# Tying the loads, sums and stores of attention merges behind later work in a two-layer trunk kernel

## The chip, the cores and the metric

One core of one Trainium2 chip. The metric is device microseconds of one execution, as the median of several runs. Five engines work side by side: PE (matrix products), DVE (vector), ACT (scalar, activations), POOL (GpSimd) and SP, which here issues every DMA on one queue, in order.

## The reference

Two layers over 1024 rows of width 1024. Layer 0 is dilated attention, and only it is touched here; layer 1 (grouped attention with sinks) follows.

```python
def mixer_a(x, w_in, w_out, cos, sin):
    h = x @ w_in
    for gi, (window, dil) in enumerate(((128, 1), (512, 4), (2048, 16))):
        q, k, v = split_cols(h[..., base:base + 3 * A_WIDTH], [A_WIDTH] * 3)
        q = apply_rope(...); k = apply_rope(...)
        o, lse = banded_attention(strided(q), strided(k), strided(v), window // dil)
        outs.append(o); lses.append(lse)
    wts = jax.nn.softmax(jnp.stack(lses, axis=0), axis=0)
    o = jnp.einsum('gbsh,gbshd->bshd', wts, jnp.stack(outs, axis=0))
    z = h[..., -A_WIDTH:]
    return (o * jax.nn.silu(z)) @ w_out
```

The softmax over the three groups and the weighted sum of their outputs are what the kernel calls a merge.

## The kernel before

Every float32 product is done as three float16 products of high and low halves (lines 272 to 274): one row tile of 128 rows against a block of 512 weight columns is 24 matmuls into a tile `lin`. A weight block comes in four chunks `wraw`, its largest value is found (`wpm` L109 on DVE, then a small table `mdd` L230, which PE spreads over the rows at L237), and ACT (L132) and DVE (L133) split it into `whl`, four instructions each.

Layer 0 works in two halves of the heads (`pair` 0 and 1). In each half the groups come in the order 1, 2, 0, and for each group one block of values and two blocks of queries with keys, eight row tiles each. A value tile leaves PSUM through ACT (`vh` L368) and DVE (`vl` L369). A query tile goes through DVE (`t` L347, L350), POOL (`t` L351), ACT (`hl` L357), POOL (`hl` L358), ACT (L361) and a DMA transpose (`qk` L362). A unit of attention takes scores on PE (`s` L385), DVE (`sm`, `mx` L389), ACT (`st` L393, `sm` L395, `phl` L399), POOL or DVE (`phl` L401), a DMA transpose (`pT` L404), PE (`o` L416 to L418) and ACT (`st` L698). There is one PSUM tile for `o`, so the next unit's `o` waits for that eviction. The result goes to a scratch array in memory (`scr` L707), with its sums and its maxima.

When the last group of a half has written row tile n, `merge(n, pair, scr)` is queued. A merge is a generator in three parts: three loads of 264 KB into `gt` (L749); then the weights, on DVE (`mM` L754, `mw` L755, `mwl`, `mL`, `mw` L758 to L762) with one ACT exponential (`mw` L756) and three POOL instructions over 512 columns (`gt` L765 to L767); then two DVE instructions (L769, L770) and the store `oa` (L771). `merge_step` moves it on; at most two merges are under way, and `gt` has two buffers. There are eight merges in each half. Those of pair 0 fall into the end of its last group and the first group of pair 1. Those of pair 1 fall into its last query block and into the z blocks (gate columns; `zt`, `zu` L720 to L723, store `za` L729) which end the layer. Behind these comes the output projection: its weights `wo` are split (L132, L133) once the last store has left `gt`'s memory, and then `wg`, the weights of the next gate, are loaded and measured.

The order of instructions on each engine is not written out by hand. The framework's scheduler decides it from the program order and its own estimates, and an engine keeps that order: an instruction that waits holds up all behind it. `issue_after(ins)` adds one demand to it: what is issued inside stands behind `ins` on its engine.

Of the kernel before, what the change touches and what calls it, by code (L numbers as in the profile page):

```python
# [15 lines left out]
ALU = mybir.AluOpType  # L16
AX = mybir.AxisListType
# [3 lines left out]
P = 128  # L21
# [5 lines left out]
HD = 64  # L27
# [6 lines left out]
V_SHIFT = 25  # L34
# [105 lines left out]
class Trunk:  # L140
# [196 lines left out]
    def rope_out(self, ps, nq, nk, n, dst):  # L337

        nc, w = self.nc, self.work
        nh = nq + nk
        t1 = w.tile([P, 512], F32, tag="t1", name="t1")
        t2 = w.tile([P, 512], F32, tag="t2", name="t2")
        pv = ps.rearrange("p (h c) -> p h c", c=32)
        cos = self.cos[:, n, :].unsqueeze(1).to_broadcast([P, 2 * nh, 32])
        nc.vector.tensor_mul(t1[:, :nh * HD].rearrange("p (h c) -> p h c", c=32), pv, cos)  # L347
        pb = ps.rearrange("p (h b c) -> p h b c", b=2, c=32)[:, :, ::-1, :]
        sin = self.sin[:, n].unsqueeze(1).to_broadcast([P, nh, 2, 32])
        nc.vector.tensor_mul(t2[:, :nh * HD].rearrange("p (h b c) -> p h b c", b=2, c=32), pb, sin)  # L350
        nc.gpsimd.tensor_add(t1[:, :nh * HD], t1[:, :nh * HD], t2[:, :nh * HD])  # L351
        nb = nh + nk
        hl = w.tile([P, 12, P], F16, tag="hl", name="hl", bufs=3)
        rv = t1[:, :nh * HD].rearrange("p (h c) -> p h c", c=HD)

        def parts():
            nc.scalar.activation(hl[:, :nh, 0:HD], rv, AF.Copy)  # L357
            nc.gpsimd.tensor_sub(hl[:, :nh, HD:P], rv, hl[:, :nh, 0:HD])  # L358
            if nk:
                src, to = (hl[:, a:b, :].rearrange("p h (w c) -> p h w c", w=2) for a, b in ((nq, nh), (nh, nb)))  # L360
                nc.scalar.activation(to, src[:, :, ::-1, :], AF.Copy)  # L361
            nc.sync.dma_start(dst, hl[:, :nb, :].rearrange("p b c -> p (b c)"), transpose=True)  # L362

        self.ends.append(parts)

    def v_out(self, ps, vh, vl):
        nc = self.nc
        nc.scalar.activation(vh, ps, AF.Copy, scale=2.0 ** -V_SHIFT)  # L368
        nc.vector.scalar_tensor_tensor(vl, ps, 2.0 ** -V_SHIFT, vh, op0=ALU.mult, op1=ALU.subtract)  # L369


    def scores(self, qa, kas, mask, cs, ncs, sums, nbias, floor, pool_lo):

        nc, at = self.nc, self.att
        nb = len(kas)
        nk = nb * P
        sm = at.tile([P, 4, 2 * P], F32, tag="sm", name="sm", bufs=self.bufs)
        mx = self.small.tile([P, 4], F32, tag="mx", name="mx", bufs=6)
        for pr in range(2):
            ps = self.ps_s.tile([P, 2, 2 * P], F32, tag="s", name="s")  # L380
            for i in range(2):
                h = 2 * pr + i
                for kb, ka in enumerate(kas):
                    for sw in range(2):
                        nc.tensor.matmul(ps[:, i, kb * P:(kb + 1) * P], qa(h), ka(h, sw), start=(sw == 0),  # L385
                                         stop=(sw == 1))
            for i in range(2):
                h = 2 * pr + i
                nc.vector.tensor_tensor_reduce(sm[:, h, :nk], ps[:, i, :nk], mask, 1.0, -3e38, ALU.add, ALU.max,  # L389
                                               mx[:, h:h + 1])  # L390
        if floor is not None:
            nc.vector.tensor_max(mx, mx, floor)
        nc.scalar.activation(nbias, mx, AF.Copy, scale=ncs, bias=LN_PSCALE)  # L393
        for h in range(4):
            nc.scalar.activation(sm[:, h, :nk], sm[:, h, :nk], AF.Exp, bias=nbias[:, h:h + 1], scale=cs,  # L395
                                 accum_out=sums[:, h:h + 1])
        pf = at.tile([P, 16 * P], F16, tag="phl", name="phl", bufs=self.bufs)
        hl = pf[:, :8 * nk].rearrange("p (a h c) -> p a h c", a=2, h=4)
        nc.scalar.activation(hl[:, 0], sm[:, :, :nk], AF.Copy)  # L399
        eng = nc.gpsimd if pool_lo else nc.vector  # L400
        eng.tensor_sub(hl[:, 1], sm[:, :, :nk], hl[:, 0])  # L401
        pt = at.tile([P, 2, 4, 2, P], F16, tag="pT", name="pT", bufs=len(self.pipe))
        ptf = pt.rearrange("p a h b c -> p (a h b) c")[:, :8 * nb, :]
        nc.sync.dma_start(ptf, pf[:, :8 * nk], transpose=True)  # L404
        return ptf.rearrange("p (a h b) c -> p a h b c", a=2, h=4)

    def pv(self, pt, va, vla):
# [308 lines left out]
    def z_rows(self, pool, ps, c):  # L716

        nc = self.nc
        t = pool.tile([P, 512], F32, tag="t1", name="zt")
        nc.scalar.activation(t, ps, AF.Tanh, scale=c)  # L720
        u = pool.tile([P, 512], F32, tag="t2", name="zu")
        nc.scalar.activation(u, ps, AF.Copy, scale=c)  # L722
        nc.vector.scalar_tensor_tensor(u, t, 1.0, u, op0=ALU.add, op1=ALU.mult)  # L723
        return u

    def z_tile(self, pool, n, half):
# [17 lines left out]
    def merge(self, n, pair, scr):  # L744

        nc, at, sp = self.nc, self.att, self.small
        gt = at.tile([P, 3, 2, 4 * HD + 8], F32, tag="gt", name="gt")
        for g in range(3):
            nc.sync.dma_start(gt[:, g], scr[g][n * P:(n + 1) * P])  # L749
        sums, nb = gt[:, :, :, 4 * HD:4 * HD + 4], gt[:, :, :, 4 * HD + 4:]  # L750
        yield
        w = sp.tile([P, 3, 2, 4], F32, tag="mw", name="mw")
        M = sp.tile([P, 2, 4], F32, tag="mM", name="mM")
        nc.vector.tensor_reduce(M, nb.rearrange("p g a h -> p a h g"), axis=AX.X, op=ALU.min)  # L754
        nc.vector.tensor_sub(w, M.unsqueeze(1).to_broadcast([P, 3, 2, 4]), nb)  # L755
        nc.scalar.activation(w, w, AF.Exp)  # L756
        wl = sp.tile([P, 3, 2, 4], F32, tag="mwl", name="mwl")
        nc.vector.tensor_mul(wl, w, sums)  # L758
        L = sp.tile([P, 2, 4], F32, tag="mL", name="mL")
        nc.vector.tensor_reduce(L, wl.rearrange("p g a h -> p a h g"), axis=AX.X, op=ALU.add)  # L760
        nc.vector.reciprocal(L, L)
        nc.vector.tensor_mul(w, w, L.unsqueeze(1).to_broadcast([P, 3, 2, 4]))  # L762
        x = [gt[:, g, :, 0:4 * HD].rearrange("p a (h c) -> p a h c", c=HD) for g in range(3)]
        wb = [w[:, g].unsqueeze(3).to_broadcast([P, 2, 4, HD]) for g in range(3)]
        nc.gpsimd.tensor_mul(x[1], x[1], wb[1])  # L765
        nc.gpsimd.tensor_mul(x[2], x[2], wb[2])
        nc.gpsimd.tensor_add(x[1], x[1], x[2])  # L767
        yield
        nc.vector.tensor_mul(x[0], x[0], wb[0])  # L769
        nc.vector.tensor_add(x[0], x[0], x[1])  # L770
        nc.sync.dma_start(self.o_dr[n][:, pair * 512:(pair + 1) * 512].rearrange("p (a c) -> p a c", a=2),  # L771
                          gt[:, 0, :, 0:4 * HD])

    def merge_step(self):

# [372 lines left out]
```

## Time and profile before

| | |
|---|---|
| runs | 1655.76, 1656.32, 1660.85 us; median 1656.32 |
| profiled execution | 1658.17 us, of which the trace's span is 1656.4 |
| PE busy | 1587.8 us (96%) |
| DVE, ACT, POOL busy | 1078.1 (65%), 922.7 (56%), 664.6 us (40%) |
| mean granted clock of PE | 0.985 |

PE is busy nearly all the time, so the engines' shares say little: the time is PE's work, plus PE's waits, plus what a lower granted clock adds. A wait is read from the idle time ahead of a PE instruction and the name of what released it, and a lower clock from the distance between one matmul's start and the next.

### The profile page before, as it was taken

To read this page: it belongs to the slowest core of one execution; us is meant where nothing else is said; L and a number is where in the kernel's file an instruction comes from. 1 tells how busy PE (TensorE), PEld (TensorE's weight loads), DVE (VectorE), ACT (ScalarE), POOL (GpSimd) and SP (SyncE) were. 2 spreads that over 40 slices of the span, in tenths; PEclk is the share of its full clock that TensorE was granted. 3 is DMA by queue.
4 is the path that set the end of the run, shared out by engine and by line. 5 is a ranking of instruction groups with operands and counts; after the bars stand their busy time and mean duration, and the time that the engine had idled before them with its cause. 6 is when DMAs were issued, how large, how long until landed. Compare 5 with 4: busy or idle time off the path is not lost. (4 is left out here: it accounts for less than half of the span.)

```text
span 1656.4 us, 29029 instructions
## 1 busy us (share of the span) xinstructions
PE 1587.8 (96%) x10579; PEld 883.2 (53%) x10579; DVE 1078.1 (65%) x2619; ACT 922.7 (56%) x2050; POOL 664.6 (40%) x477
## 2 busy tenths in 40 slices
PE   9999999999999799999999988899999998999998
PEld 3455676654555456666545543344455555544444
DVE  6866655655566776556466567887447998677731
ACT  4537665675774467656657843533334878754321
POOL 0015624532554665155235653453323452225341
PEclk9999999999999999999999998999999999999999
DMA  9718867775887777567658885989975898998963
GB/s 362 251 61 172 186 135 149 153 158 126 164 159 203 207 170 159 127 157 163 142 124 187 190 226 202 336 221 264 248 185 113 155 206 183 189 297 215 262 197 109
DMA packets 543792, 311.02 MB, mean 188 GB/s; under 512 B 473120, under 2 KB 494240, under 8 KB 543392
## 3 DMA queue, kind: packets, MB, share of 16 engines
q1 hardware_dynamic: 543648, 309.16, 75.3%
q8 instruction: 83, 1.36, 0.3%
q14 instruction: 61, 0.50, 0.1%
HBM read 137.78 MB, written 54.92 MB: 116 GB/s over the span
## 5 line engine op out<-in xcount | busy, mean ns | idle before, releaser
L272 PE MATMUL lin<-whl,xhl 128*128 128x512 f16 x1280 | 488.5, 382 | 2.6 <-ACT zu L722 2.6
L273 PE MATMUL lin<-whl,xhl 128*128 128x512 f16 x1280 | 488.7, 382 | 0.0
L274 PE MATMUL lin<-whl,xhl 128*128 128x512 f16 x1280 | 488.7, 382 | 0.0
L351 POOL TENSOR_TENSOR t<-t,t 128x512 f32<-128x512 f32 (+1 forms) x120 | 153.4, 1278 | 284.8 <-DVE t L350 268.0
L401 POOL TENSOR_TENSOR phl<-sm,phl 128x1024 f16<-128x1024 f32 (+1 forms) x88 | 155.6, 1769 | 233.3 <-ACT phl L399 205.9
L109 DVE TENSOR_REDUCE wpm<-wraw 128x1 f32<-128x1024 f32 (+1 forms) x132 | 156.8, 1197 | 93.6 <-DMA wraw<-in_wa_dram 54.8
L274 PEld LDWEIGHTS <-xhl 128*128 128x128 f16 x1280 | 149.3, 117 | 127.5 <-issue 3.5
L273 PEld LDWEIGHTS <-xhl 128*128 128x128 f16 x1280 | 149.7, 117 | 119.5 <-issue 6.7
L272 PEld LDWEIGHTS <-xhl 128*128 128x128 f16 x1280 | 149.4, 117 | 119.7 <-issue 3.8
L395 ACT ACTIVATE sm<-sm,st,cs 128x128 f32<-128x128 f32 (+1 forms) x384 | 203.6, 532 | 3.6 <-ACT st L393 0.4
L358 POOL TENSOR_TENSOR hl<-t,hl 128x512 f16<-128x512 f32 (+1 forms) x120 | 145.3, 1211 | 131.7 <-ACT hl L357 131.7
L389 DVE CUSTOM_DVE_ANT_0 sm<-s,tab 128x256 f32<-128x256 f32 (+1 forms) x512 | 157.0, 358 | 31.5 <-PE s L385 23.0
L133 DVE SCALAR_TENSOR_TENSOR whl<-wraw,s,whl 128x1024 f16<-128x1024 f32 (+1 forms) x116 | 168.3, 1501 | 12.8 <-ACT whl L132 12.8
L357 ACT ACTIVATE hl<-t 128x512 f16<-128x512 f32 (+1 forms) x120 | 72.3, 602 | 125.4 <-POOL t L351 124.0
L347 DVE TENSOR_TENSOR t<-lin,rope 128x512 f32<-128x512 f32 (+1 forms) x120 | 78.9, 657 | 75.7 <-PE lin L274 41.6
L132 ACT ACTIVATE whl<-wraw,s 128x1024 f16<-128x1024 f32 (+1 forms) x116 | 121.8, 1122 | 5.1 <-DVE s L212 5.0
L272 PE MATMUL lin<-whl,x2T 128*128 128x512 f16 (+1 forms) x320 | 115.5, 361 | 0.0
L273 PE MATMUL lin<-whl,x2T 128*128 128x512 f16 (+1 forms) x320 | 115.2, 360 | 0.0
L274 PE MATMUL lin<-whl,x2T 128*128 128x512 f16 (+1 forms) x320 | 115.0, 359 | 0.0
L399 ACT ACTIVATE phl<-sm 128x1024 f16<-128x1024 f32 (+1 forms) x128 | 110.2, 861 | 1.2
L361 ACT ACTIVATE hl<-hl 128x512 f16<-128x512 f16 (+1 forms) x104 | 63.2, 608 | 54.2 <-POOL hl L358 53.9
L385 PE MATMUL s<-qk 128*128 128x128 f16 x1120 | 81.5, 220 | 9.1 <-DMA qk<-hl 9.1
(187 smaller groups left out, 2883.5 us busy)
## 6 DMA issues: line engine op xcount, KB each, us to landing
wraw<-in_wa_dram SPq DMA_DIRECT2D x56, 512.0 KB, 6.0
scr<-st SPq DMA_DIRECT2D x96, 132.0 KB, 2.3
gt<-scr SPq DMA_DIRECT2D x48, 264.0 KB, 3.4
wraw<-in_wav_dram SPq DMA_DIRECT2D x24, 512.0 KB, 6.4
prh<-pro SPq DMA_DIRECT2D x32, 256.0 KB, 4.1
wraw<-in_wg_dram SPq DMA_DIRECT2D x16, 512.0 KB, 8.7
wraw<-in_wb_dram SPq DMA_DIRECT2D x16, 512.0 KB, 6.4
xg<-y SPq DMA_DIRECT2D x16, 512.0 KB, 3.6
```

The source lines that it names most:

```text
L109: k.nc.vector.tensor_reduce(pm[:, c:c + 1], self.raw[:, c * q:(c + 1) * q], axis=AX.X, op=ALU.max, apply_absolute_value=True)
L132: nc.scalar.activation(hl[:, 0, sl], self.raw[:, sl], AF.Copy, scale=self.s)
L133: self.last = nc.vector.scalar_tensor_tensor(hl[:, 1, sl], self.raw[:, sl], self.s, hl[:, 0, sl], op0=ALU.mult, op1=ALU.subtract)
L272: mm(ps, xh(kt), wh, start=(kt == 0), stop=False)
L273: mm(ps, xh(kt), wl, start=False, stop=False)
L274: mm(ps, xl(kt), wh, start=False, stop=(kt == NK - 1))
L351: nc.gpsimd.tensor_add(t1[:, :nh * HD], t1[:, :nh * HD], t2[:, :nh * HD])
L358: nc.gpsimd.tensor_sub(hl[:, :nh, HD:P], rv, hl[:, :nh, 0:HD])
L389: nc.vector.tensor_tensor_reduce(sm[:, h, :nk], ps[:, i, :nk], mask, 1.0, -3e38, ALU.add, ALU.max, mx[:, h:h + 1])
L395: nc.scalar.activation(sm[:, h, :nk], sm[:, h, :nk], AF.Exp, bias=nbias[:, h:h + 1], scale=cs, accum_out=sums[:, h:h + 1])
L399: nc.scalar.activation(hl[:, 0], sm[:, :, :nk], AF.Copy)
L401: eng.tensor_sub(hl[:, 1], sm[:, :, :nk], hl[:, 0])
```

## The change

The kernel now remembers the latest DMA transpose it has issued (`moved`) and the latest DVE eviction of a value, query or z tile (`evicted`). A merge's three loads are ordered behind the first, and its first DVE instruction behind the second. For pair 0 a merge gets one part more: its store comes a step later, and behind the latest transpose of that time.

```diff
@@ rope_out
-        nc.vector.tensor_mul(t2[:, :nh * HD].rearrange("p (h b c) -> p h b c", b=2, c=32), pb, sin)
+        self.evicted = nc.vector.tensor_mul(t2[:, :nh * HD].rearrange("p (h b c) -> p h b c", b=2, c=32), pb, sin)
...
-            nc.sync.dma_start(dst, hl[:, :nb, :].rearrange("p b c -> p (b c)"), transpose=True)
+            self.moved = nc.sync.dma_start(dst, hl[:, :nb, :].rearrange("p b c -> p (b c)"), transpose=True)
@@ v_out
-        nc.vector.scalar_tensor_tensor(vl, ps, 2.0 ** -V_SHIFT, vh, op0=ALU.mult, op1=ALU.subtract)
+        self.evicted = nc.vector.scalar_tensor_tensor(vl, ps, 2.0 ** -V_SHIFT, vh, op0=ALU.mult, op1=ALU.subtract)
@@ scores
-        nc.sync.dma_start(ptf, pf[:, :8 * nk], transpose=True)
+        self.moved = nc.sync.dma_start(ptf, pf[:, :8 * nk], transpose=True)
@@ z_rows
-        nc.vector.scalar_tensor_tensor(u, t, 1.0, u, op0=ALU.add, op1=ALU.mult)
+        self.evicted = nc.vector.scalar_tensor_tensor(u, t, 1.0, u, op0=ALU.add, op1=ALU.mult)
@@ merge
-        for g in range(3):
-            nc.sync.dma_start(gt[:, g], scr[g][n * P:(n + 1) * P])
+        with self.tc.issue_after(self.moved.ins):
+            for g in range(3):
+                nc.sync.dma_start(gt[:, g], scr[g][n * P:(n + 1) * P])
...
-        nc.vector.tensor_reduce(M, nb.rearrange("p g a h -> p a h g"), axis=AX.X, op=ALU.min)
+        with self.tc.issue_after(self.evicted.ins):
+            nc.vector.tensor_reduce(M, nb.rearrange("p g a h -> p a h g"), axis=AX.X, op=ALU.min)
...
-        nc.sync.dma_start(self.o_dr[n][:, pair * 512:(pair + 1) * 512].rearrange("p (a c) -> p a c", a=2),
-                          gt[:, 0, :, 0:4 * HD])
+        if pair == 0:
+            yield
+        with self.tc.issue_after(self.moved.ins) if pair == 0 else nullcontext():
+            nc.sync.dma_start(self.o_dr[n][:, pair * 512:(pair + 1) * 512].rearrange("p (a c) -> p a c", a=2),
+                              gt[:, 0, :, 0:4 * HD])
```

Added lines move the later numbers: L749 is L750 after, L756 is L758, L765 to L767 are L767 to L769, L771 is L776, L898 is L903.

**SP's queue where pair 0's merges begin.** Shown as a difference, before with - and after with +; `pT` are transposes of attention units, `scr` stores of theirs.

```order
 L404 DMA_TRANSPOSE pT_5648<-phl_5645 128x16x128
 L707 DMA scr0_0_615<-st_5417 128x264
-L771 DMA oa0_599<-gt_5748 128x2x256
-L749 DMA gt_6390<-scr0_0_615 128x528
-L749 DMA gt_6390<-scr1_0_616 128x528
-L749 DMA gt_6390<-scr2_0_617 128x528
-L771 DMA oa1_600<-gt_5752 128x2x256
 L404 DMA_TRANSPOSE pT_5746<-phl_5743 128x16x128
+L750 DMA gt_5748<-scr0_0_615 128x528
+L750 DMA gt_5748<-scr1_0_616 128x528
+L750 DMA gt_5748<-scr2_0_617 128x528
```

The first merges' loads and stores stood between two transposes and now stand behind the later one, six loads in a row; the first store, `oa0`, comes several transposes further on. There are four such bursts for pair 0, two merges each, where before the eight merges followed one another from the first of these places.

**ACT and POOL at the end of that value block.** ACT first, as a difference, at the change from the value block to the first query block of the last group of pair 0; then POOL's rows of after at the same place.

```order
 L395 ACTIVATE sm_5935,st_5934<-sm_5935,st_5934,cs54_4770 128x256 x4
+L758 ACTIVATE mw_5977<-mw_5977 128x24
+L758 ACTIVATE mw_5991<-mw_5991 128x24
 L399 ACTIVATE phl_5964<-sm_5935 128x1024
-L756 ACTIVATE mw_7362<-mw_7362 128x24
 L368 ACTIVATE vh_646<-lin_6013 128x2x256
 L132 ACTIVATE whl_6109<-wraw_5111,s59_6009 128x1024 x4
 L698 ACTIVATE st_5713<-o_78,cv45_3731 128x256
-L756 ACTIVATE mw_7376<-mw_7376 128x24
 L357 ACTIVATE hl_6104<-t1_6099 128x8x64
```

```order
L401 TENSOR_TENSOR phl_5859<-sm_5830,phl_5859 128x1024
L767 TENSOR_TENSOR gt_5748<-gt_5748,mw_5977 128x2x256
L401 TENSOR_TENSOR phl_5964<-sm_5935,phl_5964 128x1024
L768 TENSOR_TENSOR gt_5748<-gt_5748,mw_5977 128x2x256
L767 TENSOR_TENSOR gt_5752<-gt_5752,mw_5991 128x2x256
L768 TENSOR_TENSOR gt_5752<-gt_5752,mw_5991 128x2x256
L769 TENSOR_TENSOR gt_5748<-gt_5748 128x2x256
L769 TENSOR_TENSOR gt_5752<-gt_5752 128x2x256
L351 TENSOR_TENSOR t1_6099<-t1_6099,t2_6100 128x512
```

Here no merge's exponential stands any longer between `phl` and the split `whl`, nor between `st` and `hl`; the two first ones stand together ahead of a `phl`. On POOL all six products of two merges stand ahead of the first query tile's `t`. The same pattern returns once, where pair 1's first value block ends; the two other bursts stand between query tiles.

**SP's queue at the end of the z blocks.** Before first, then after, from the store of the last z tile of the first half of z to the first load of the output projection (`ot`); `gt_11610` is the last merge.

```order
L729 DMA za7_614<-zu_11552 128x512
L771 DMA oa5_604<-gt_11457 128x2x256
L749 DMA gt_11610<-scr0_1_618 128x528
L749 DMA gt_11610<-scr1_1_619 128x528
L749 DMA gt_11610<-scr2_1_620 128x528
L102 DMA wraw_11693<-in_wg_dram 128x1024 x2
L729 DMA za0_607<-zu_11592 128x512
L102 DMA wraw_11693<-in_wg_dram 128x1024 x2
L729 DMA za1_608<-zu_11683 128x512
L771 DMA oa6_605<-gt_11559 128x2x256
L771 DMA oa7_606<-gt_11610 128x2x256
L729 DMA za2_609<-zu_11728 128x512
```

```order
L102 DMA wraw_11693<-in_wg_dram 128x1024 x4
L729 DMA za1_608<-zu_11683 128x512
L776 DMA oa5_604<-gt_11457 128x2x256
L729 DMA za2_609<-zu_11728 128x512
L750 DMA gt_11610<-scr0_1_618 128x528
L750 DMA gt_11610<-scr1_1_619 128x528
L750 DMA gt_11610<-scr2_1_620 128x528
L776 DMA oa6_605<-gt_11559 128x2x256
L729 DMA za3_610<-zu_11780 128x512
L729 DMA za4_611<-zu_11825 128x512
L776 DMA oa7_606<-gt_11610 128x2x256
L893 DMA g_b_11644<-in_lng_dram 128x1024
```

The last merge's loads have moved from ahead of the `wg` load and of z tile 0's store to behind both and behind z tile 2's store; its own store has moved from ahead of z tile 2's to behind z tile 4's.

## Rows read from the trace of the kernel before

**Rows 1.** Waits of PE, 505 to 585 us: total, times, longest.

```profile
PE o L416 <- ACT st L698: 7.6, 3, 4.4
PE s L385 <- DMA qk<-hl: 4.6, 2, 3.1
```

**Rows 2.** Timeline of PE: start, duration, instruction, idle before and its releaser.

```profile
520.11 0.38 PE L272 MATMUL lin<-whl,xhl 128*128 128x512 f16 x1
...
520.75 0.38 PE L272 MATMUL lin<-whl,xhl 128*128 128x512 f16 x1
...
551.35 0.21 PE L416 MATMUL o<-vh,pT 128*128 128x64 f16 x1 [4.45 <-ACT st L698]
```

**Rows 3.** Windows: length, busy time by engine, granted clock, DMA share, GB/s.

```profile
520.00:540.00 20.00, 17.83 (x130) 10.18 (x129) 13.76 (x38) 8.94 (x25) 14.41 (x10) 0.91 0.74 188
540.00:560.00 20.00, 15.55 (x82) 7.92 (x81) 14.68 (x24) 9.10 (x19) 9.33 (x7) 0.83 0.68 165
```

**Rows 4.** Waits of ACT, 505 to 585 us.

```profile
ACT mw L756 <- DVE mw L755: 24.3, 8, 8.5
```

**Rows 5.** Timeline of ACT at the end of the value block.

```profile
546.69 4.25 ACT L132 ACTIVATE whl<-wraw,s 128x1024 f16<-128x1024 f32 x4
550.85 0.46 ACT L698 ACTIVATE st<-o,cv 128x256 f32<-128x256 f32 x1
```

**Rows 6.** Timeline of DVE at the same place.

```profile
544.21 0.18 DVE L754 TENSOR_REDUCE mM<-gt 128x8 f32<-128x24 f32 x1 [1.60 <-DMA gt<-scr]
...
549.38 4.87 DVE L133 SCALAR_TENSOR_TENSOR whl<-wraw,s,whl 128x1024 f16<-128x1024 f32 x3
```

**Rows 7.** Waits of SP's DMA queue, 505 to 585 us.

```profile
SPq L362 <- ACT mw L756: 6.1, 2, 4.1
```

**Rows 8.** Timeline of ACT at a block change without merges.

```profile
696.37 4.27 ACT L132 ACTIVATE whl<-wraw,s 128x1024 f16<-128x1024 f32 x4
```

**Rows 9.** Timeline of DVE at that block change.

```profile
696.50 0.69 DVE L369 SCALAR_TENSOR_TENSOR vl<-lin,vh 128x512 f16<-128x512 f32 x1 [3.76 <-ACT vh L368]
697.54 4.87 DVE L133 SCALAR_TENSOR_TENSOR whl<-wraw,s,whl 128x1024 f16<-128x1024 f32 x4 [0.35 <-ACT whl L132]
```

**Rows 10.** Timeline of POOL at that block change.

```profile
694.84 2.14 POOL L401 TENSOR_TENSOR phl<-sm,phl 128x1024 f16<-128x1024 f32 x1 [6.70 <-ACT phl L399]
703.69 1.27 POOL L351 TENSOR_TENSOR t<-t,t 128x512 f32<-128x512 f32 x1 [6.71 <-DVE t L350]
```

**Rows 11.** Timeline of PE at the first scores behind that block change.

```profile
712.47 0.62 PE L385 MATMUL s<-qk 128*128 128x128 f16 x8 [0.56 <-DMA qk<-hl]
```

**Rows 12.** Groups by line, whole program: busy us, mean ns, idle before.

```profile
L765 POOL TENSOR_TENSOR gt<-gt,mw 128x512 f32<-128x512 f32 x16 | 23.6, 1477 | 58.3 <-DVE mw L762 56.7 <-DMA gt<-scr 1.3
L767 POOL TENSOR_TENSOR gt<-gt 128x512 f32<-128x512 f32 x16 | 21.6, 1347 | 1.2
L766 POOL TENSOR_TENSOR gt<-gt,mw 128x512 f32<-128x512 f32 x16 | 19.4, 1212 | 0.0
```

**Rows 13.** Waits of PE, 940 to 1145 us.

```profile
PE s L237 <- DVE mdd L230: 12.2, 2, 7.3
...
PE o L416 <- DMA pT<-phl: 3.7, 1, 3.7
...
PE s L385 <- DMA qk<-hl: 1.5, 1, 1.5
```

**Rows 14.** Timeline of PE in the second half of z.

```profile
1016.48 0.38 PE L272 MATMUL lin<-whl,xhl 128*128 128x512 f16 x1 [2.59 <-ACT zu L722]
```

**Rows 15.** Timeline of PE at the second of the two `mdd` waits.

```profile
1054.14 0.29 PE L237 MATMUL s<-mdd,ones 128*128 128x128 bf16 x1 [7.33 <-DVE mdd L230]
```

**Rows 16.** Timeline of SP's DMA queue: the last merges' loads and stores.

```profile
1007.97 1.27 SPq L749 DMA_DIRECT2D gt<-scr  x3
...
1023.95 3.42 SPq L771 DMA_DIRECT2D oa<-gt  x2
```

**Rows 17.** Timeline of DVE: the last merge's first instruction.

```profile
1014.56 0.18 DVE L754 TENSOR_REDUCE mM<-gt 128x8 f32<-128x24 f32 x1 [4.94 <-DMA gt<-scr]
```

## The prediction

> **What bounds the kernel now.** PE is the bound, so I read first what PE itself waits for, then the engines it waits on. From 505 to 585 us, where pair 0's merges run, PE waits three times for the eviction `st` of the attention sums and twice for a transposed query tile, 12.2 us together [rows 1]; the longest, 4.45 us, stands at the end of the last value block [rows 2]. The waits also cost clock: the granted clock is 0.91 and 0.83 in these two stretches of 20 us [rows 3], a mix of full speed (2.4 GHz) and half (1.2 GHz), each fall behind a wait. That is 1.8 + 3.4 = 5.2 us of full speed at most; half of the 4.45 us wait, 2.2, may sit in it and cost nothing, so 3.0 at least. I take 4.0. The stretch thus loses about **16.2 us**.
>
> Why `st` is late is read on ACT. Its merge exponentials `mw` wait 24.3 us in eight waits, the longest 8.5 [rows 4], for DVE's `mw`, which in turn stands behind the merge's loads [rows 6]. ACT goes on in order, so the wait hits whatever stands behind. At the long wait of PE the four `whl` splits run from 546.69 to 550.9 and `st` only at 550.85 [rows 5]; PE starts its `o` at 551.35. The query transposes wait on the same exponential, 6.1 us twice over [rows 7].
>
> The comparison is a block change of the same kind without merges. There ACT's `whl` runs just as long, 4.27 us [rows 8], DVE has 3.76 us idle ahead of its `vl` [rows 9], POOL idles 6.70 us and 6.71 us on both sides of its `phl` [rows 10], and PE's first scores wait only 0.56 us [rows 11].
>
> **The change, part by part.**
>
> *Removed.* In the order of after, the exponentials of pair 0 stand at four places, two together, behind score work or query work that is done anyway, and their loads stand behind an early transpose, several steps ahead of the sums. So neither the loads nor the sums should be late, and ACT no longer holds `st`, `vh` and `whl`. I count the whole 16.2 us as recovered: −16.2. The small DVE instructions of the two merges fall into idle time like the 3.76 us of [rows 9]; without that cover they would add about that much to DVE, which has no deadline there before `whl`.
>
> *Added.* Six POOL instructions stand ahead of the first query tile's `t` at two of the four places. One merge is 1.48 + 1.21 + 1.35 = 4.04 us [rows 12], two are 8.1. The first L765 stands ahead of the unit's `phl`, the other five, 8.1 − 1.5 = 6.6 us, fit the 6.71 us of [rows 10] only if `phl` isn't later than there. But the first L765 waits for ACT's exponentials, which stand just ahead of ACT's `phl`, so `phl` on POOL comes later by up to that instruction, 1.5 us, and if DVE's `whl` lengthens the POOL work the excess is larger: from 0 to about 3 us a place. I take 2, and there is nothing to hide it, since the first scores already wait 0.56 us [rows 11]: two places, **+4**. At the other two places the merges stand between query tiles, whose transposes only the first tiles need at once; 0 to 1, taken as nothing.
>
> *Loads in bursts.* Six loads (1.6 MB) stand together on SP. Three of them take 1.27 us to issue where nothing holds them [rows 16], so six take some 2.6, and a transpose behind them would be that much late at worst; it stands at least two units ahead of the products that need it in this order. Nothing. The stores, a step later, hold `gt` longer; the next two merges aren't due before the next burst. Nothing, and if that were wrong it would delay a merge that no one in the first half waits for.
>
> *End of layer 0.* Pair 1's merges and the z blocks show these waits of PE: for `qk` 1.5 and `pT` 3.7 [rows 13], for `zu` 2.59 [rows 14], for the tables `mdd` 12.2 in two waits [rows 13], the second of 7.33 at 1054.14 [rows 15]. The first two come where the first merges' POOL and DVE work crowds an attention unit; the order puts these merges later. With the clock, half of 4.0 for one such pair of waits, they cost about 7; between nothing and that, I take 5 as gained, since the `pT` wait is the one whose `phl` now has POOL to itself.
>
> But the last `mdd` hangs on a chain: last merge's loads at 1007.97, sums at 1014.56 [rows 17], stores at 1023.95 and 3.42 us on [rows 16], then the split of `wo`, the load of `wg`, its maxima, `mdd`, and PE at 1054.14. In the order of after the last loads stand behind z tile 2's store. A z tile is 24 matmuls at (520.75 − 520.11)/3 = 0.213 us [rows 2], 5.1 us. Tile 2 would, without its wait, begin at 1016.48 − 2.59 = 1013.9, end at 1019.0, and be stored some 2 us later: loads at about 1021. With as long to the sums (1014.56 − 1007.97 = 6.6) and from there to the store (about 1027 − 1014.6 = 12.4) the last store comes at 1040 instead of 1027: 13 us later at the worst. At best 0, since the two merges no longer run into each other and the table ahead of the first `mdd` wait has been moved in front of the last sums. I take 6. All of these times move earlier with whatever PE gains upstream, so the end of layer 0 gives −5 + 6 = **+1**, with −12 and +13 as ends.
>
> *Sum.* 1658.17 − 16.2 + 4 + 1 = 1647.0 on the profiled execution, which lay 1.85 us above the median of the runs, 1656.32. On the median that is 1645.1; I say **1646**.
>
> **Rivals.**
>
> *The end gains as well.* If the last store is not late, the waits of the z blocks go too: of 12.2 + 3.7 + 2.6 + 1.5 = 20 us [rows 13, 14] about half, with their clock. For it: the z tiles' evictions lose the exponential that held them. Against it: the last merge stands later on every engine. 1645 − 1 − 10 = 1634.
>
> *The last merge's chain is too late.* By order the last store has moved three z tiles back, from ahead of tile 2's to behind tile 4's. If PE's tiles pass no faster than before, that is 3 × 5.1 = 15.4 us on the way to the second `mdd`, plus 2 for the clock behind a longer wait, half of the 4.0 above. 1656.3 − 12.2 + 17.4 = 1661.5: slower. Against it: between tiles 0 and 3 PE itself waited, so tiles pass faster now. It decides from 17 us of delay at 1054.14 onward.
>
> *DVE and POOL hold each other up.* At the value block's end DVE's `whl` now stands beside five POOL products. Beside two such products, three `whl` took 4.87 us, 1.62 each [rows 6]; alone, four took 4.87, 1.22 each [rows 9]. By these rows four cost 1.6 us more, 3.2 for both places, part of it hidden. If instead each of the four waited out a whole POOL product, 1.35 us [rows 12], that is 5.4 a place, 10.8 for both, which are lost entirely if PE has no slack there: 1645.1 + 10.8 − (the 4 already counted) = 1652. That is the other reading of the same row: 1.62 is a mean over three, of which perhaps one only met a product.
>
> The Trainium skill, page "SBUF — State Buffer", section "Who interferes with whom", states this second reading: a DVE instruction with two inputs in SBUF contends with a GpSimd instruction that reads SBUF, and of the two that share the pair of ports one gets it for the whole instruction while the other is fully blocked. By that rule the time would be near the 1652 of this rival; the trace shows a lengthening of 0.4 us per instruction, less than the length of a POOL product.
>
> *The change does nothing.* New waits of the same size could take the old ones' places, for instance when sums tied behind an eviction still stand ahead of a `phl` that PE needs: 1656.
>
> **How the numbers follow.** The main case 0.57 (1640 to 1652), the end gains too 0.14 (1634), DVE against POOL 0.13 (1652), no effect 0.07 (1656), the chain too late 0.09 (1661.5). What a measurement of this kernel can tell from no change is 0.3%, 5 us: faster is below 1651.4, slower above 1661.3. The main case is faster in 0.54 of 0.57; with the second case and some of the third that is 0.70; slower is the last case and what bad ends add to it, 0.10; the rest, 0.20, is the same. The range leaves out 0.07 below, half of the gaining case, and 0.12 above: 1634 to 1658.
>
> **What would show it.** Right: between 505 and 585 us ACT has no wait of more than 1 us at the exponential, PE none for `st`, and the clock is 1.00 there; a wait of 1 to 3 us for `qk` at the first scores behind two value blocks, POOL's `t` late there behind the merge's products. The second `mdd` wait of PE as long as before or longer, the first shorter. Wrong: a new wait of PE for `st` or `qk` of 4 us or more at any of the four places, `whl` instructions of 2 us and more beside POOL, or PE reaching the second `mdd` table over 10 us later than the gain upstream allows.

## The result and the profile after

The changed kernel takes 1679.75 us (1675.27 to 1681.43, 5 runs), the kernel before 1659.32 beside it (5 runs): ratio 1.0124 [1.0107, 1.0142]. It is slower by 20 us; I had said 1646 and "faster". The profiled execution took 1675.27 us, its span is 1673.5, so it is compared with a span of 1656.4: 17.1 us.

PE's busy time has not grown (1584.7 us against 1587.8), so the time is again waits and clock. I read PE's waits first, in the three stretches in which the change acts: the first half's first merges (505 to 585), its later ones (660 to 830) and the end of layer 0 (940 to 1170).

```profile
PE s L385 <- DMA qk<-hl: 4.9, 1, 4.9
PE o L416 <- ACT st L698: 2.2, 1, 2.2
...
PE o L416 <- ACT st L698: 8.4, 3, 4.9
PE s L385 <- DMA qk<-hl: 4.2, 1, 4.2
...
PE s L237 <- DVE mdd L230: 29.6, 2, 21.1
```

Of [rows 1]'s 12.2 us, 7.1 are back under other causes, at one place: the change from the value block to the queries. 12.6 us of waits for `st` and `qk` are new between 660 and 830 us, where before the block change had the 0.56 of [rows 11]. At the end of the layer the two `mdd` waits, 12.2 us in [rows 13], are 29.6. The windows show the same with the clock (columns as in [rows 3]):

```profile
520.00:540.00 20.00, 20.00 (x148) 11.60 (x147) 11.14 (x39) 13.74 (x31) 7.67 (x5) 1.00 0.59 148
540.00:560.00 20.00, 12.89 (x101) 7.30 (x99) 18.39 (x26) 4.67 (x12) 13.84 (x9) 0.81 0.64 179
700.00:720.00 20.00, 10.92 (x64) 6.68 (x63) 17.74 (x27) 6.19 (x16) 12.08 (x8) 0.74 0.62 173
...
1060.00:1080.00 20.00, 2.36 (x6) 0.85 (x7) 19.47 (x39) 12.17 (x16) 6.52 (x5) 0.50 1.05 287
```

The first window was at 0.91 and lost 2.2 us of PE; now it is full. So the change does what it says: ACT no longer holds PE while the value block runs. The next windows give it back.

To add these up I compare when the same `lin` tile starts in the two traces; the difference grows only where time is lost. By this shift (after less before) the changed kernel is 10.9 us ahead at the end of the value block (tile 82), 6.8 ahead behind the block change (85), 4.4 behind past the second one (107) and 4.9 from the next tile on, 10.0 behind past a wait at 804.88 us (122), 7.1 behind ahead of the end of the z blocks (157), 23.3 past the second `mdd` wait (160), and 17.1 at the end.

**A block change, engine by engine.** The timeline: SP's queue, then ACT, DVE, POOL and PE at the first one, then four rows of the second.

```profile
522.32 2.95 SPq L750 DMA_DIRECT2D gt<-scr  x6
525.37 0.38 SPq L707 DMA_DIRECT2D scr<-st  x1
...
530.90 0.30 ACT L393 ACTIVATE st<-mx,ncs 128x4 f32<-128x4 f32 x1 [4.31 <-DMA scr<-st]
...
550.31 0.63 ACT L357 ACTIVATE hl<-t 128x512 f16<-128x512 f32 x1 [10.10 <-POOL t L351]
550.84 0.46 ACT L698 ACTIVATE st<-o,cv 128x256 f32<-128x256 f32 x1
...
537.73 8.51 DVE L133 SCALAR_TENSOR_TENSOR whl<-wraw,s,whl 128x1024 f16<-128x1024 f32 x4
...
539.16 2.03 POOL L768 TENSOR_TENSOR gt<-gt,mw 128x512 f32<-128x512 f32 x1
541.15 2.02 POOL L767 TENSOR_TENSOR gt<-gt,mw 128x512 f32<-128x512 f32 x1
...
548.55 1.72 POOL L351 TENSOR_TENSOR t<-t,t 128x512 f32<-128x512 f32 x1
...
551.35 0.19 PE L416 MATMUL o<-vh,pT 128*128 128x64 f16 x1 [2.19 <-ACT st L698]
557.13 1.04 PE L385 MATMUL s<-qk 128*128 128x128 f16 x8 [4.92 <-DMA qk<-hl]
...
689.16 0.30 ACT L393 ACTIVATE st<-mx,ncs 128x4 f32<-128x4 f32 x1 [6.71 <-DMA scr<-st]
695.98 8.52 DVE L133 SCALAR_TENSOR_TENSOR whl<-wraw,s,whl 128x1024 f16<-128x1024 f32 x4
709.58 0.21 PE L416 MATMUL o<-vh,pT 128*128 128x64 f16 x1 [4.92 <-ACT st L698]
715.18 1.03 PE L385 MATMUL s<-qk 128*128 128x128 f16 x8 [4.16 <-DMA qk<-hl]
```

Two things are to be seen. DVE's four `whl` take 8.51 us, 2.13 each, against 4.87 in [rows 9]; POOL's products beside them take 2.02 to 2.03 us each, against the means of [rows 12]. Both are late for the first query tile, `t` starts at 548.55, and ACT, which goes on in order, waits 10.10 us at `hl` with `st` behind it: PE's `o` hangs on a query tile with which it has nothing to do. And ahead of all that, the six loads keep SP busy for 2.95 us with a unit's store `scr` behind them; the two stores of units there take 4.1 us to land, as a median, against 2.4 over the whole program, probably because their data stand behind the loads' too (argued; no run shows it apart). ACT's next `st` needs the buffer that this store reads, and ACT waits 4.31 us (6.71 at the second change) with `vh` and `whl` behind it.

**The end of layer 0.** SP's queue, then DVE and PE:

```profile
1033.23 1.34 SPq L750 DMA_DIRECT2D gt<-scr  x3
...
1044.54 0.37 SPq L776 DMA_DIRECT2D oa<-gt  x1
...
1052.83 2.74 SPq L102 DMA_DIRECT2D wraw<-in_wg_dram  x4
...
1074.55 0.28 DVE L230 TENSOR_SCALAR mdd<-tab,mde 128x128 bf16<-128x128 f32 x1
...
1074.90 0.29 PE L237 MATMUL s<-mdd,ones 128*128 128x128 bf16 x1 [21.15 <-DVE mdd L230]
1077.93 0.59 PE L272 MATMUL lin<-whl,ogT 128*128 128x512 f16 x1 [2.74 <-DMA ogT<-rhl]
```

The last merge's loads come at 1033.23 (1007.97 in [rows 16]), its store at 1044.54. In before, the last store is the second of the pair in [rows 16]; by itself it is

```profile
1027.00 0.37 SPq L771 DMA_DIRECT2D oa<-gt  x1
```

So the store is 17.5 us later, which is 10.6 more than PE's own tiles are there (6.9 behind at tile 159). The chain behind it is longer too: from the store to PE's start at the table it takes 30.4 us, and 27.1 in before, and the first product behind the table then waits another 2.7 us for its transposed operand `ogT`. DVE's order differs there: in after, the weight split `whl` of the output projection starts ahead of the maxima `wpm` of `wg`, and in before, it stands behind `mdd`. After first, then before:

```profile
1060.87 4.13 DVE L133 SCALAR_TENSOR_TENSOR whl<-wraw,s,whl 128x1024 f16<-128x1024 f32 x2 [0.29 <-ACT whl L132]
1064.93 1.21 DVE L109 TENSOR_REDUCE wpm<-wraw 128x1 f32<-128x1024 f32 x1
```

```profile
1053.80 0.29 DVE L230 TENSOR_SCALAR mdd<-tab,mde 128x128 bf16<-128x128 f32 x1
...
1054.67 1.27 DVE L133 SCALAR_TENSOR_TENSOR whl<-wraw,s,whl 128x1024 f16<-128x1024 f32 x1
```

### The profile page after: what moved, and what is told of

The parts are those of the page before. It is cut to its first block, busy times and chain, and to the rows that moved or that the text cites. A ratio compares the mean times of both kernels' runs of the same rounds, so it can differ in the third digit from the quotient of the medians.

```text
span 1673.5 us, 29018 instructions
## 1 busy us (share of the span) xinstructions
PE 1584.7 (95%) x10579; PEld 882.0 (53%) x10579; DVE 1098.7 (66%) x2619; ACT 923.2 (55%) x2050; POOL 671.7 (40%) x477
## 4 chain that ended last, share of the span: by engine, by line
PE 52%; DVE 11%; DMA 11%; POOL 7%; ACT 6%; issue 6%; SPq 3%; POOLq 0%; DVEq 0%; ACTq 0%
PE lin L272 15%; PE lin L274 15%; PE lin L273 15%; DVE whl L133 4%; PE s L385 3%; ACT sm L395 2%; DMA pT<-phl 2%; DMA gt<-scr 1%; ACT whl L132 1%; DMA wraw<-in_wb_dram 1%; POOL phl L401 1%; POOL t L351 1%; DVE sm L389 1%; POOL hl L358 1%; POOL og L907 1%
## 5 line engine op out<-in xcount | busy, mean ns | idle before, releaser
L133 DVE SCALAR_TENSOR_TENSOR whl<-wraw,s,whl 128x1024 f16<-128x1024 f32 (+1 forms) x116 | 175.8, 1566 | 16.0 <-ACT whl L132 15.9
```

Of the source, the lines that this page charges most:

```text
L133: self.last = nc.vector.scalar_tensor_tensor(hl[:, 1, sl], self.raw[:, sl], self.s, hl[:, 0, sl], op0=ALU.mult, op1=ALU.subtract)
```

## The experiments

My theory now had four parts: (1) DVE and POOL hold each other up at the block changes; (2) the burst of loads delays `scr`, so ACT; (3) a further wait at 804.88 us; (4) at the end, the last merge's store is late. Against it stood: the store that comes a step later, or the tied sums themselves; and for the end, that the waits are only upstream lateness. Twelve kernels were run, each with the kernel before on the same chip.

**The two halves apart.** `first_half` has the ties for pair 0 alone, `second_half` for pair 1 alone.

```diff
-        with self.tc.issue_after(self.moved.ins):
+        with self.tc.issue_after(self.moved.ins) if pair == 0 else nullcontext():
...
-        with self.tc.issue_after(self.evicted.ins):
+        with self.tc.issue_after(self.evicted.ins) if pair == 0 else nullcontext():
```

> Only pair 0's merges are tied (loads, sums, later store); pair 1's are as before. Theory A, that the loss sits at two places, the two block changes where DVE's weight split meets POOL's merge products, and the chain of the last merge: the first half stands as in the changed kernel, which is 10 us late when the third query stage begins, and the end of layer 0 as in the kernel before: 1664 to 1670 us, waits of PE for st and qk of 2 to 5 us at both block changes, whl at about 2.1 us each there, and PE's two mdd waits of 5 and 7 us as before. Rival, that the tail alone loses and the first half gains: 1640 to 1648.

> Only pair 1's merges are tied (loads and sums); pair 0's are as before. Theory A: the waits from 505 to 585 us as before (12 us), and at the end of layer 0 the last store behind z tile 4's, PE's second mdd wait near 21 us, clock at half for over 20 us: 1665 to 1671. Rival, that the long mdd wait comes from the first half's lateness: mdd waits as before, 1655 to 1660.

`first_half`: 1667.87 us, ratio 1.0059 [1.0034, 1.0085]. `second_half`: 1669.46, 1.0079 [1.0052, 1.0107]. Against 1656.8 that is 11 and 13 us, and the ratios' excesses sum to 0.0138, inside the interval of the full change. Each half does its own damage: `second_half` has no new wait in the first half and still waits 21.3 us for the second `mdd`. The traces differ by up to 4.3 us ahead of tile 70, where none of the edits acts, so from here on I read what a shift gains or loses between two tiles and not the shift itself.

**Where the first half loses.** `hold_first` lets no merge take a step in the last three tiles of pair 1's value blocks, so the products leave the block changes; `late_first` keeps only the later store of pair 0; `first_nopool` leaves out POOL's three products of pair 0's merges; `first_dve` has these three on DVE.

```diff
+                    self.hold = pair == 1 and n >= 5   # hold_first, around progress() in the value blocks
...
+        if pair:                                       # first_nopool
             nc.gpsimd.tensor_mul(x[1], x[1], wb[1])
...
+        (nc.gpsimd if pair else nc.vector).tensor_mul(x[1], x[1], wb[1])   # first_dve
```

> As first_half, but merges take no step during the last three tiles of a value block of pair 1, so that their POOL products come between query tiles and not beside the split of the next block's weights. Theory A: whl back at 1.2 us each, no wait for st or qk over 1 us at these two block changes, 1640 to 1649 us. Rival, that the bursts of six loads or the ties themselves hold the queues up wherever they stand: waits of the same size move with the merges, 1660 or more.

> Of the change only this: pair 0's store a step later and behind the latest transpose; loads and sums untied. In the order its products come in the middle of value blocks, two merges together, and no exponential stands ahead of the split. Theory A: what counts is where the products stand, so this too takes the waits from 505 to 585 us away without the collision: 1641 to 1651 us. Rival, that the tied loads are what takes the waits away: 1655 to 1660.

> As first_half, but pair 0's merges leave out their three POOL products, so its rows of the output are not the full sums; loads, exponentials, DVE's part and stores stay where they were. Theory A, that DVE's split and POOL's products hold each other up: whl at 1.2 to 1.35 us each at both block changes instead of 2.1, no wait for st there, a wait for the first qk of at most 4 us at the first; 1648 to 1656 us. Rival, that the bursts of loads or the exponentials slow the split: whl stays at 2 us and the time at 1663 or more.

> As first_half, but pair 0's three products are on DVE instead of POOL. Theory A: nothing contends, whl back at 1.2 to 1.35 us each, but DVE has 4 us more to do ahead of or between them, so the first query tile's t comes about as late as in first_half, while POOL is free for it: no wait for st over 1 us, for the first qk 3 to 5 us; 1654 to 1662 us. Rival, that it is the amount of merge work ahead of the query tile that counts and not the engine pair: as first_half, 1664 to 1670.

| | us | ratio |
|---|---|---|
| `hold_first` | 1652.47 | 0.9978 [0.9959, 0.9997] |
| `late_first` | 1656.69 | 1.0000 [0.9985, 1.0016] |
| `first_nopool` | 1655.09 | 0.9990 [0.9979, 1.0001] |
| `first_dve` | 1660.12 | 1.0016 [1.0004, 1.0029] |

`late_first` ends where before does, and not at the 1641 to 1651 us that I had expected. With no load or sum tied it gains 8.3 us between tiles 70 and 85, and gives them back in waits for `qk` of 6.7 and 4.4 us at the two block changes, with no product beside `whl`. So the later store costs nothing in the sum, but not for want of effects.

`hold_first` turns the loss of the first half into a small gain, with the ties kept. I had expected no wait above 1 us at the block changes; at the first one PE still waits 4.2 us for `qk`, though no `whl` is longer than 1.80 us there:

```profile
PE s L386 <- DMA qk<-hl: 4.2, 1, 4.2
```

Without POOL's products DVE's `whl` falls back to its old length, and PE waits 0.2 us for `st`, yet 10.4 us for `qk` remain; DVE's row, then the waits of PE (505 to 730 us) and of ACT (505 to 550) in `first_nopool`:

```profile
540.34 4.86 DVE L133 SCALAR_TENSOR_TENSOR whl<-wraw,s,whl 128x1024 f16<-128x1024 f32 x4
...
PE s L385 <- DMA qk<-hl: 10.4, 2, 6.0
PE o L416 <- ACT st L698: 0.2, 1, 0.2
...
ACT st L393 <- DMA scr<-st: 3.9, 1, 3.9
```

In `first_dve` the products take DVE's time instead, and `whl` shows that the length depended on POOL: the same four instructions, 1.24 to 1.27 us each, pushed back but hardly stretched (the fourth, not shown, is like the third).

```profile
544.04 2.47 DVE L133 SCALAR_TENSOR_TENSOR whl<-wraw,s,whl 128x1024 f16<-128x1024 f32 x2
...
547.03 1.27 DVE L133 SCALAR_TENSOR_TENSOR whl<-wraw,s,whl 128x1024 f16<-128x1024 f32 x1
```

(The order of `first_dve` on PE is not that of `first_half`: at both changes the first scores stand behind more of the block's products. So its time prices nothing.)

So part (1) is shown as a mechanism. It is not yet what PE loses: at the first change PE waits 6.0 us in `first_nopool` against 6.5 in `first_half` (1.8 and 4.7), at the second 4.3 against 8.7 (4.9 and 3.8).

**The burst.** `first_g0` is `first_nopool` with one group's load in a merge in place of three (its merges of pair 0 compute with that group alone; the small instructions shrink too). Six loads in a row become two.

```diff
+        G = 3 if pair else 1
...
-            for g in range(3):
+            for g in range(G):
                 nc.sync.dma_start(gt[:, g], scr[g][n * P:(n + 1) * P])
```

> As first_nopool, but pair 0's merges also load only one of the three groups, so its output rows are those of one group; a burst on SP is two loads of 264 KB instead of six. Theory A, extended by what first_nopool left (first qk 6.1 and 4.3 us late at the two block changes): the burst delays the store scr behind it, ACT's next st waits for that buffer 4 to 7 us, and the split, the query tile and its transpose are that much later. Then ACT's wait for scr is under 2 us here, the qk waits of PE under 2 us, 1640 to 1648 us. Rival, that the qk wait comes from the weight loads beside the transpose: qk waits of 4 us and more stay, 1652 to 1656.

1649.19 us, ratio 0.9949 [0.9932, 0.9966]. ACT's wait for `scr` at the first change is gone (3.9 us in `first_nopool`) and is 1.8 us at the second (4.9), and PE's waits for `qk` are 4.8 us for both changes:

```profile
PE s L385 <- DMA qk<-hl: 4.8, 2, 3.2
```

The first of them, 3.22 us, is more than I expected. It goes with how early DVE begins `whl`, measured back from the time at which PE is ready for the first scores (their start less their wait): 10.2 us ahead in `first_nopool` (wait 6.05), 12.6 in `first_g0` (3.22), 14.4 in [rows 9, 11] (0.56). `first_g0` closes about half of that distance at the first change, so the burst, or the small merge work that shrank with it, is shown as a cause, and not as the only one there. The rest is open. The traces point at DVE's part of the two merges (L771, L772): with it in between, DVE begins `whl` 4.4 us behind ACT in `first_nopool` and 3.2 in `first_g0`, against 1.2 in `slots_b` (below). No run takes it away by itself.

The shifts give the prices. From tile 82 to 85 (first change) and from 106 to 108 (second), `first_half` loses 6.7 and 10.7 us against `slots_b`, `first_nopool` 6.2 and 6.2, `first_g0` 3.5 and 0.7. So the products are worth 0.5 us at the first change, where the query tile would have been late without them, and 4.5 at the second; the loads with the small work are worth 2.7 and 5.5. No run takes the loads away and leaves the products, so this split goes by the order of removal.

**The wait at 804.88 us.** It stands in `first_half` too, at 801.19, 3.4 us, and moves PE's tiles there from +1.1 to +6.3 us against before. The trace of `first_half` suggested a chain: two merges' products on POOL, DVE's last addition of a merge waiting for them, the maxima `mx` behind it, ACT waiting 4.33 us for these. `first_no67` leaves out the products of the last two merges of pair 0 alone.

```diff
+        if pair or n < 6:
             nc.gpsimd.tensor_mul(x[1], x[1], wb[1])
...
```

> The first half's ties alone (pair 1 as before), but the last two merges of pair 0 leave out POOL's three products each (so its output lacks two groups there); the six others keep them. Question: the wait of PE for st at 801 us, 3.4 us with its clock, which shifts PE's tiles from +0.6 to +6.3 us against before. If POOL's products of these two merges cause it (DVE's last addition of a merge waits for them and stands ahead of the maxima mx, for which ACT's st waited 4.33 us): the wait near 800 us falls below 1.5 us, both block changes stay as in the run with the first half's ties (4.9 and 3.8 us at the second), and the time is about 5 us below that run's, 1662 to 1663. If the burst's loads or the exponentials cause it: 3 us of wait stay there and the time stays near 1668.

1660.96 us, ratio 1.0017 [0.9997, 1.0036], 0.42% below `first_half`. The wait is gone, and the block changes are as in `first_half` (4.93 and 3.92 us at the second). ACT's waits, 760 to 803 us, first of `first_half`, then of `first_no67`:

```profile
ACT st L393 <- DVE mx L389: 4.7, 2, 4.3
...
ACT mw L758 <- DVE mw L757: 3.5, 2, 1.9
```

```profile
ACT mw L758 <- DVE mw L757: 3.0, 2, 1.9
...
ACT st L393 <- DVE mx L389: 0.2, 1, 0.2
```

The exponentials' waits at `mw` are unchanged, 3.5 and 3.0 us, and the wait for `mx` is gone: the products cause it, not the loads. Part (3) is shown.

**The end of layer 0, in doses.** `second_n0_only` ties the loads of pair 1's first merge alone, `second_sums` only the sums of pair 1's merges.

```diff
+        with self.tc.issue_after(self.moved.ins) if pair == 1 and n == 0 else nullcontext():   # second_n0_only
...
+        with self.tc.issue_after(self.evicted.ins) if pair == 1 else nullcontext():            # second_sums
```

> Only the loads of pair 1's first merge are tied. In the order its two buffers pass the lateness on: the last merge's loads stand behind z tile 1's store and its own store behind tile 3's, each one tile earlier than in second_half. Theory A, that PE's second mdd wait follows the place of the last store: it is 5 to 11 us shorter than second_half's 21 us, and the time 1660 to 1666. Rival, that the other ties (sums, seven more loads) make the tail slow: 1655 to 1659.

> Only the sums of pair 1 are tied, not the loads. In the order the last merge's loads stay where they are before, behind the last z tile of the first half of z, and its store comes one z tile later than before, behind tile 2's. Theory A: PE's second mdd wait 7 to 12 us, 1655 to 1662. Rival, that tied sums cost as much as tied loads: 1665 or more.

`second_n0_only`: 1668.81 us, ratio 1.0074 [1.0056, 1.0091]; `second_sums`: 1663.30, 1.0031 [1.0014, 1.0049]. Both are above what I had expected (1660 to 1666 and 1655 to 1662). PE's waits from 1000 to 1090 us, of `second_half`, of `second_n0_only` (with two rows of its timeline) and of `second_sums`:

```profile
PE s L237 <- DVE mdd L230: 29.8, 2, 21.3
```

```profile
PE lin L272 <- issue: 16.0, 1, 16.0
...
1056.73 0.58 PE L272 MATMUL lin<-whl,ogT 128*128 128x512 f16 x1 [16.01 <-issue]
...
1084.96 0.22 PE L237 MATMUL s<-mdd,ones 128*128 128x128 bf16 x1
```

```profile
PE s L237 <- DVE mdd L230: 17.4, 2, 11.8
```

The 16.0 us are another wait: in `second_n0_only` the first product of the output projection stands ahead of the table's matmul on PE, and the profile names no releaser for it. By the order of SP's queue the last merge's store stands ahead of z tile 2's store in before, and behind z tile 2's, 3's and 4's in `second_sums`, `second_n0_only` and `second_half`. PE's longest wait there is 7.33 [rows 15], 11.8, 16.0 and 21.3 us, 4.6 us more for each z tile on average.

But the store is not all of it. In `second_sums`, `second_n0_only` and `second_half` it comes at 1028.02, 1029.06 and 1039.27 us; against PE's tiles (tile 159) that is 1.2, 8.2 and 10.6 us later than in before. From it to the first product of the output projection it takes 31.0, 27.7 and 33.0 us, and 27.7 in before. So the late store is the whole delay at this place in `second_n0_only`, two thirds of it in `second_half`, and about a quarter in `second_sums`; the rest is the longer chain behind the store, with DVE's order as above in `second_half`. Nothing was run on that chain by itself.

Tying one merge's loads, the first of eight, costs nearly as much as tying all (though in part further on, in two waits for `ogT` of 4.7 and 3.0 us, which are 3.1 and 1.1 in before): `gt` has two buffers, so a merge that starts late hands its lateness to the one after next, and so on to the last. Part (4) is shown as far as the store goes; the longer chain is read from the traces alone.

**One merge at a time.** The two last runs keep the ties of pair 0 and change where its merges take their steps: one merge at a time, a step each at tiles 1, 3, 5, 7 (`slots`) or 0, 2, 4, 6 (`slots_b`) of every block of pair 1. Pair 1's merges are as before.

```diff
-        self.merge_wait -= 1
-        if self.merge_wait > 0:
-            return
-        self.merge_wait = self.merge_every
-        while len(self.merging) < 2 and self.merges:
+        at = (0, 2, 4, 6)
+        if self.slot is not None:
+            if self.slot not in at:
+                return
...
+        while len(self.merging) < (2 if self.slot is None else int(self.slot == at[0])) and self.merges:
```

> Pair 0's merges tied as in the change, but one at a time, a step at every second row tile of pair 1 (tiles 1, 3, 5, 7 of each block: loads, sums, end, store), so bursts are three loads and no POOL product comes at a block change; pair 1 as before. Theory A: no wait of PE over 1.5 us between 505 and 800 us, 1641 to 1648. Rival, that eight places with half the merge work each cost as much as four with two: 1652 to 1658.

> As slots, a tile earlier (tiles 0, 2, 4, 6): the loads come at the first tile of each block, beside the weight loads and the first transpose, the store ahead of the block change. Theory A: like slots but with the loads at a busier place, waits for qk or pT of 1 to 3 us at some blocks: 1643 to 1652. Rival: as before, 1655 to 1660.

`slots`: 1653.13 us, ratio 0.9977 [0.9961, 0.9993]. `slots_b`: **1644.35** us (1642.49 to 1647.86, 6 runs), 0.9926 [0.9910, 0.9941], faster than both kernels. I had expected the odd tiles to do better, because a merge's loads then stay away from a block's first tile; they didn't: `slots` has waits of 1.7 and 3.0 us at the block changes and 4.2 us for `st` between and behind them, `slots_b` of 1.4 and 0.9. Its waits of PE (505 to 830 us) and two windows:

```profile
PE s L386 <- DMA qk<-hl: 2.3, 2, 1.4
```

```profile
520.00:540.00 20.00, 20.00 (x148) 11.58 (x147) 10.90 (x31) 13.94 (x30) 5.69 (x3) 1.00 0.39 95
540.00:560.00 20.00, 18.61 (x142) 10.83 (x141) 15.25 (x32) 7.68 (x19) 8.31 (x7) 1.00 0.80 217
```

Here `whl` takes 4.87 us, DVE begins it 14.6 us ahead of the time at which PE is ready, and PE is 16.4 us ahead of before at tile 100 and still 15.3 at tile 156. The same slots without the ties give the order of before, instruction for instruction, on every engine: the ties are what makes the scheduler keep a place at all, and the place is what decides.

## Why the prediction was wrong

*Removed, −16.2: right in mechanism and size.* `slots_b`, which has pair 0's ties and little of their side effects (waits of 1.4 and 0.9 us), gains 16.4 us by tile 100. In the changed kernel itself the gain stood for a few tiles: −10.9 at tile 82, ahead of the last of [rows 1]'s waits. (The 6.1 us of [rows 7] are two waits together, not "6.1 us twice over"; no term uses them.)

*Added, +4: this step failed.* Against the clean stage, the first block change costs about 8 us (−6.8 in place of −15.0 at tile 85; `first_half` with the same ties 6.7), the second 11.7 (−6.8 to +4.9) and the wait at 804.88 us 5.1 (to +10.0): 25 in place of 4. I had added up POOL's products and set them against POOL's idle time, one engine alone. Three things were missing.

First, **DVE and POOL hold each other up**, the rival to which I gave 0.13. I took 1.62 us for a `whl` beside products as "a lengthening of 0.4"; it was a mean over three. The trace of before shows the three apart, in ns, shortest, median and longest:

```profile
L133 DVE SCALAR_TENSOR_TENSOR whl<-wraw,s,whl x3: 1272/1456/2287, 549.4 to 553.0; 128x1024 f16<-128x1024 f32 x3
```

The price of one meeting, 2.29 us, could be read there; 2.13 was measured. Four cost 8.51 − 4.86 = 3.7 us more at each change, between the 1.6 of the first reading and the 5.4 of the second, and POOL's products lengthen by nearly as much, which the rival left out. That is time of DVE and POOL. PE gets back 0.5 and 4.5 us of it when the products go, since the burst and the merges' small work make the same query tile late. The rule of the Trainium skill's page "SBUF — State Buffer", section "Who interferes with whom", that I set beside it, an exclusive lock between DVE and GpSimd, agrees: a `whl` and a product together take 2.0 to 2.1 us, close to the sum of 1.22 and 1.04, the shortest product of `slots_b` and `first_half`, one that meets no `whl`.

Second, I followed the late `t` to `qk` alone. On ACT, an `st` stands right behind `hl` (550.31 and 550.84 above; the order in the text on the change ends at `hl`, one instruction short of it), so one late query tile makes PE wait twice, 2.19 + 4.92 and 4.92 + 4.16 us.

Third, "the other two places … taken as nothing": at the last of them the products held DVE's addition, this held `mx`, and that cost 5.1 us. POOL's rows there were followed to `t`, not to DVE.

*Loads in bursts, nothing: failed.* The burst's length was right (2.95 us, I had worked out 2.6). I asked only which transposes stand behind it. What stood behind it was a store of 132 KB whose buffer ACT needs: 4.31 and 6.71 us of ACT, just ahead of `vh` and `whl`. *Stores a step later, nothing: right* in the sum of `late_first`, not in its parts.

*End of layer 0, +1: mis-sized, and the rival "the last merge's chain" came true.* Alone it costs 12.7 us (`second_half`); in the full change the shift goes from 7.1 to 23.3 us between tiles 157 and 160, of which 6 are given back by the end. What gives them back was not tested; the trace has none of the three waits that stand behind the table in before (3.1, 1.2 and 1.1 us, from 1111 to 1137). The last store was three z tiles late, as I had read from the order, and I had worked out 13 us as the upper end. I took 6, about halfway; against the rival I had held that tiles "pass faster now". The store shows how little that helped: it came 10.6 us later than PE's tiles. And I had left the chain behind the store as long as it was, where it grew by 5.7 us up to the first product, 3.2 of them ahead of the table. My condition, 17 us of delay at 1054.14, is met (20.8), but the rival's price was too low: it put 17.4 us of wait in place of 12.2, and 29.6 were measured, since the first `mdd` wait grew too (8.48 against 4.89), where I had said it would shrink. The −5 for the waits at `pT` and `qk` came to about −3 (the shift goes from 10.0 to 7.1 between tiles 122 and 157), and not by the `pT` wait, on which I had rested it: `pT` is 5.0 us there against 3.7, while `qk` with 1.5 and `zu` with 2.6 are gone.

The three signs that I had named for "wrong" all appeared: waits for `st` or `qk` above 4 us, `whl` above 2 us beside POOL, and PE over 10 us late at the second table. In shifts, the sum reads −15.0 (the gain, as `slots_b` shows it at tile 85) + 8.2 + 11.7 + 5.1 + 7.1 (from 10.0 at tile 122 to 17.1 at the end) = 17 us where I had −16.2 + 4 + 1.

## What to carry to other kernels

When instructions are moved behind something, follow every engine's queue at the new place to the next two instructions behind them, and ask whose buffer each waits for: here a query tile held an unrelated eviction, and a load burst held a store that held ACT. Instructions that are gathered to clear one place become a burst at another; the same ties with one merge at a time gained 13 us at one set of tiles and 4 at another, where two at a time lost 11 in the first half. A wait that stays when its cause is taken out has a second cause right behind the first, so what a removal gives back is less than what the cause takes up on its engine. And in a ring of two buffers a delay of the first user reaches the last one, so a tie at a place without a deadline must be traced to the end of the ring.

## What the runs showed of the hardware

DVE's `whl` (two operands, 1024 columns, 1.22 us) and POOL's products (512 columns, 1.04 us at the shortest) took 2.13 and 2.02 us each while both ran, four and three in a row: the pair took about as long as the two alone, one after the other (2.26 us). Without POOL's products the four took 4.86 us, and 1.24 to 1.27 each with the products on DVE. The window from 1060 to 1080 us, the end of PE's wait of 21.15 us and 5 us behind it, was granted half the clock (0.50, 1.2 GHz). PE's matmuls behind the wait started 0.43 us apart up to 1081.3 and 0.21 to 0.22 from 1081.6 on, so the wait's price went beyond itself.
